# A hybrid attention block on one core: another order ahead of the first projection and around the first up unit, forget rows by one DMA, biases behind the first attention

## The chip, the cores and the metric

The kernel runs on one core of one Trainium2 chip. The metric is the device time of one execution in microseconds (us); lower is better. Every time below is of one launch with all inputs in DRAM.

## The reference

One layer over 256 tokens of width 1024, batch 1, all in float32. What is computed:

```python
h = rmsnorm(x, norm_mix)
proj = einsum('bsd,de->bse', h, w_in)          # q, k, v of three branches, 8 forget logits, 3 gates
o_a = stick_breaking_attention(q_a, k_a, v_a)  # 8 heads of 64
o_b = forgetting_attention(q_b, k_b, v_b, f_b + b_forget)   # adds c[q] - c[k], c a running sum
o_c = moba_attention(q_c, k_c, v_c, slopes)    # one block of 256 keys here: causal with ALiBi
lifted = einsum('bsnw,nwd->bsnd', branches, w_branch)
mixed = sum(sigmoid(g) * lifted, axis=branches)
x = x + mixed @ w_out
h = rmsnorm(x, norm_mlp)
hid = square(relu(h @ w_up))                   # 4096 features
x = x + hid @ w_down
out = rmsnorm(x, norm_final)
```

## The kernel before, in words

**Products.** Each float32 operand is split into a high part (`hi`, the value copied to the matmul's reduced float type) and a low part (`lo`, the rest), and a product is the sum of hi*hi, hi*lo and lo*hi. A weight tile is made in three steps by `pump` (L104): a DMA on SyncE's queue brings 1 MB into `raw` (two buffers), ScalarE (ACT) copies each half to `whi` (L122), VectorE (DVE) subtracts for `wlo` (L125). There are seven buffers of each, so `pump` runs up to seven halves ahead of `used` (L132), which TensorE's stages call when a half is spent. The first two halves are made otherwise: GpSimd (POOL) makes `whi_qa` of both (L124), DVE the first `wlo_qa`, POOL the second (L125).

**Order.** Up to the end of `proj_first` the program runs in the order in which it is written (`manual_schedule`). Behind it a scheduler orders each engine by what is ready in its model and by the order of the code; `follow` (L137) adds an edge that only keeps two instructions of one engine in order.

**Ahead of the first projection (L190 to L300).** TensorE runs twelve matmuls on zeros (L196) while the inputs load. For each of the two token tiles t = 0, 1, ACT and DVE sum squares (L232, L233), POOL takes the root (L246), and then DVE scales half of the tile (L278) and ACT the other half (L279). TensorE transposes the gains (L283) and then the scaled tiles, two feature blocks at a time and both token tiles of a block in turn (L288 to L293), and ACT and DVE write `hT` from the transposed blocks: hi by `gain_hi` (L256), lo by `gain_lo` (L260), eight of each. `proj_first` (L337) then runs 48 matmuls of 256 columns; the next stage is the `k` projection, `pqk<-hT,whi_ka`.

**Attention.** The steps of the three branches are interleaved by a table of events (L578 to L585) with the projections. `forget_terms` (L473) makes the running sums c, sends them to DRAM (`c_rows`, L498), and `forget_bias` (L508) brings two heads' rows back to all partitions by two DMAs of 128 KB (L513) and makes the biases of these two heads: ACT adds the row term (L519, four instructions), POOL masks (L521, four instructions). Four pairs of heads, so eight DMAs and sixteen ACT instructions. The biases are read by `softmax_pair` of branch b.

**Output projection and first up unit.** `token_major("o", ...)` (L640, called at L695) runs `part` for units u: the first four for all four output tiles, the last four (`tail`) tile by tile, so that (t, e) = (0,0), (1,0), (0,1), (1,1) come out one after another, twelve matmuls of 512 columns each. Behind each, `mixed_in` (L677) adds the residual on DVE (L681, two instructions), and `transpose_in` (L686) of the tile before runs on TensorE; with t = 1 comes `split_gain`, four `gain_hi` on ACT and four `gain_lo` on DVE into `h2`. The transposes of (1,1) stand inside the first of sixteen up units (L715), between its first sixteen matmuls (features 0 to 511) and the rest. The other up units run without a break; `token_major("d", ...)` follows, and the last norm.

The program's names: `ptr` is a transposed tile in PSUM, `pu` an up unit's sum, `ptok` a tile of a token-major projection, `x` in that stage the residual, `h` the normed activations `h2`.

Of the kernel before, what the change touches and what calls it, by code (L numbers as in the profile page):

```python
# [14 lines left out]
P = 128  # L15
S = 256
# [9 lines left out]
WARM = 12  # L26
# [11 lines left out]
def hybrid_attention_block(ctx, tc, x, norm_mix, w_in, b_forget, w_branch, w_out,  # L38
# [65 lines left out]
    def pump(up_to=None):  # L104
        while state["next"] < min(2 * len(plan), state["used"] + HALVES, up_to or 2 * len(plan)):
# [26 lines left out]
    def used(n=1):  # L132

        state["used"] += n
        pump()

    def follow(later, earlier):  # L137

        tc.add_manual_dep(later.ins, earlier.ins.name, mybir.DependencyInfo(
            mybir.DependencyClass.NoSync, mybir.DependencyReason.DATA), reason="order on one engine")  # L140
# [30 lines left out]
    def joined(p, o):  # L171

        nc.scalar.activation(p, o[:, 1], AF.Copy)
        nc.vector.tensor_tensor(p, o[:, 0], p, op=ALU.add)
# [20 lines left out]
    for i in range(WARM):  # L195
        nc.tensor.matmul(pw, idle[:, 0:P], idle, start=True, stop=True)  # L196
# [32 lines left out]
    def square_sum(src, junk, ss):  # L229

        n = src.shape[-1] // 2
        nc.scalar.activation(junk[:, 0:n], src[:, 0:n], AF.Square, accum_out=ss[:, 0:1])  # L232
        nc.vector.tensor_tensor_reduce(junk[:, n:], src[:, n:], src[:, n:], 1.0, 0.0, ALU.mult, ALU.add, ss[:, 1:2])  # L233

    def total_square(src, junk, so_far=D * EPS):
# [3 lines left out]
        square_sum(src, junk, ss)  # L239
# [14 lines left out]
    def gain_hi(pt, k0, g, hi):  # L254
        for i, k in enumerate((k0, k0 + 1)):
            nc.scalar.activation(hi[:, k], pt[:, i].rearrange("p t q -> p (t q)"), AF.Copy, scale=g[:, k:k + 1])  # L256

    def gain_lo(pt, k0, g, hi, lo):
        for i, k in enumerate((k0, k0 + 1)):
            nc.vector.scalar_tensor_tensor(lo[:, k], pt[:, i].rearrange("p t q -> p (t q)"), g[:, k:k + 1],  # L260
                                           hi[:, k].bitcast(F32), op0=ALU.mult, op1=ALU.subtract)

    def split_gain(pt, k0, g, hi, lo):
        gain_hi(pt, k0, g, hi)
        gain_lo(pt, k0, g, hi, lo)
# [5 lines left out]
    h_hi, h_lo = hT[:, :, 0], hT[:, :, 1]  # L271
    hs = []
# [508 lines left out]
```

## Time and profile before

| what | value |
|---|---|
| median of 3 runs | 461.76 us (460.93 to 462.1) |
| the profiled execution's own time | 460.2 us |
| its span, first to last instruction | 458.5 us |
| TensorE matmul (PE) | 446.5 us busy, 97% |
| VectorE (DVE) | 326.0 us, 71% |
| ScalarE (ACT) | 273.6 us, 60% |
| GpSimd (POOL) | 38.5 us, 8% |
| DMA | 80.71 MB, mean 176 GB/s |

In the rows, PE is TensorE's matmul, PEld its weight load, and SPq the DMA queue of SyncE. Times are in us from the span's start. The span is 1.7 us shorter than the execution's own time. A busy PE may still wait inside a group of matmuls; gaps between groups are listed as idle time.

### The profile page before, as it was taken

What the parts mean: (1) busy time and instruction counts of PE and PEld (TensorE: products, weight loads), DVE (VectorE), ACT (ScalarE), POOL (GpSimd) and SP (SyncE); (2) the same over time, 40 slices, a digit from 0 to 9 for tenths busy, and PEclk for the clock granted to TensorE, in tenths of its full rate; (3) what the DMA queues carried; (4) which work ended last, traced back from release to release, by engine and by line L of the source; (5) the groups of instructions that cost most, each with busy time, mean ns of one, the idle gap of its engine ahead of it and who ended that gap; (6) DMA issues with size and microseconds to landing.
All of it is one profiled execution on the core that took longest, in us unless ns stands there. A gap on an engine that the chain in (4) does not pass through costs nothing. (4 is left out here: it accounts for less than half of the span.)

```text
span 458.5 us, 6837 instructions
## 1 busy us (share of the span) xinstructions
PE 446.5 (97%) x2575; PEld 391.8 (85%) x2575; DVE 326.0 (71%) x543; ACT 273.6 (60%) x474; POOL 38.5 (8%) x75
## 2 busy tenths in 40 slices
PE   6999999999999999999999998999999999999993
PEld 3989998999899888888888887888888888888882
DVE  6878777888788878559759769877778864444425
ACT  5759997788567886556557446555556653334302
POOL 6503210213000000000000000000000000000012
PEclk9999999999999999999999999999999999999998
DMA  8768563445354448556556617766665576555202
GB/s 299 255 191 277 164 191 99 147 146 169 97 167 150 139 126 290 182 183 184 183 188 216 201 41 238 219 185 183 185 183 184 183 256 203 183 185 183 93 0 92
DMA packets 58002, 80.71 MB, mean 176 GB/s; under 512 B 2521, under 2 KB 45809, under 8 KB 57969
## 3 DMA queue, kind: packets, MB, share of 16 engines
q1 hardware_dynamic: 57632, 79.87, 54.1%
q8 instruction: 20, 0.33, 0.3%
q10 hardware_dynamic: 336, 0.40, 0.2%
q14 instruction: 14, 0.11, 0.1%
HBM read 79.21 MB, written 1.06 MB: 175 GB/s over the span
## 5 line engine op out<-in xcount | busy, mean ns | idle before, releaser
L125 DVE TENSOR_TENSOR wlo_d<-raw,whi_d 128x1024 fp32r<-128x1024 f32 x32 | 39.1, 1225 | 35.2 <-ACT whi_d L122 35.2
L151 PE MATMUL pu<-h,whi_u 128*128 128x512 f32 x256 | 61.4, 391 | 1.2 <-DVE h L260 1.2
L122 ACT ACTIVATE whi_d<-raw 128x1024 fp32r<-128x1024 f32 x32 | 33.8, 1059 | 42.3 <-PE ptok L151 34.2
L151 PEld LDWEIGHTS pu<-h,whi_u 128*128 128x128 f32 x256 | 46.9, 188 | 10.6 <-DVE h L260 1.5
L151 PE MATMUL ptok<-whi_d,u_lo 128*128 128x512 f32 x128 | 49.8, 389 | 0.0
L151 PE MATMUL ptok<-whi_d,u_hi 128*128 128x512 f32 x128 | 49.8, 389 | 0.0
L151 PE MATMUL pg<-hT,whi_g 128*128 128x512 f32 x192 | 46.7, 392 | 0.0
L122 ACT ACTIVATE whi_u<-raw 128x1024 fp32r<-128x1024 f32 x32 | 33.3, 1059 | 22.2 <-DMA raw<-in_w_up_dram 20.7
L125 DVE TENSOR_TENSOR wlo_u<-raw,whi_u 128x1024 fp32r<-128x1024 f32 x32 | 38.9, 1221 | 9.8 <-ACT whi_u L122 9.7
L151 PEld LDWEIGHTS pg<-hT,whi_g 128*128 128x128 f32 x192 | 35.1, 188 | 6.7
L125 DVE TENSOR_TENSOR wlo_g<-raw,whi_g 128x1024 fp32r<-128x1024 f32 x24 | 29.3, 1223 | 10.9 <-ACT whi_g L122 5.9
L151 PE MATMUL ptok<-wlo_d,u_hi 128*128 128x512 f32 x128 | 36.2, 389 | 0.0
L151 PEld LDWEIGHTS pu<-h,wlo_u 128*128 128x128 f32 x256 | 33.0, 191 | 1.3
L122 ACT ACTIVATE whi_g<-raw 128x1024 fp32r<-128x1024 f32 x24 | 25.4, 1058 | 14.3 <-PE pg L151 3.4
L151 PE MATMUL pu<-h,wlo_u 128*128 128x256 f32 x256 | 33.4, 283 | 0.0
L151 PEld LDWEIGHTS ptok<-whi_d,u_lo 128*128 128x128 f32 x128 | 24.0, 188 | 5.0
L151 PEld LDWEIGHTS ptok<-whi_d,u_hi 128*128 128x128 f32 x128 | 24.0, 188 | 5.0
L151 PEld LDWEIGHTS ptok<-wlo_d,u_hi 128*128 128x128 f32 x128 | 24.0, 188 | 5.0
L151 PEld LDWEIGHTS pg<-hT,wlo_g 128*128 128x128 f32 x192 | 25.1, 191 | 1.3
L151 PE MATMUL pg<-hT,wlo_g 128*128 128x256 f32 x192 | 25.5, 282 | 0.0
L739 POOL TENSOR_TENSOR xg<-x,g_fin 128x512 f32<-128x512 f32 x2 | 2.9, 1472 | 265.6 <-issue 264.2
L125 DVE TENSOR_TENSOR wlo_b<-raw,whi_b 128x1024 fp32r<-128x1024 f32 x12 | 14.7, 1223 | 10.5 <-PE pg L151 9.1
(498 smaller groups left out, 939.7 us busy)
## 6 DMA issues: line engine op xcount, KB each, us to landing
raw<-in_w_in_dram SPq DMA_DIRECT2D x29, 1024.0 KB, 5.0
raw<-in_w_up_dram SPq DMA_DIRECT2D x16, 1024.0 KB, 5.5
raw<-in_w_down_dram SPq DMA_DIRECT2D x16, 1024.0 KB, 4.8
raw<-in_w_branch_dram SPq DMA_DIRECT2D x6, 1024.0 KB, 5.0
raw<-in_w_out_dram SPq DMA_DIRECT2D x4, 1024.0 KB, 4.9
x_sb<-in_x_dram SPq DMA_DIRECT2D x2, 512.0 KB, 3.9
raw<-in_w_in_dram SPq DMA_DIRECT2D x2, 512.0 KB, 5.5
rows<-c_rows SPq DMA_DIRECT2D x8, 128.0 KB, 4.8
```

Source lines behind the costliest of these rows:

```text
L122: nc.scalar.activation(hi, raw, AF.Copy)
L125: (nc.gpsimd if n == 0 and i else nc.vector).tensor_tensor(lo, raw, hi.bitcast(F32), op=ALU.subtract)
L151: nc.tensor.matmul(o, l, r, start=first and i == 0, stop=last and i == len(pairs) - 1, **kw)
L739: nc.gpsimd.tensor_tensor(xg[:, d], x1[:, t, d], g_fin[:, d], op=ALU.mult)
```

## The change

1. **Ahead of the first projection.** Nine matmuls on zeros instead of twelve; the gains are transposed behind them, and six more matmuls on zeros stand behind that (`MORE`). The two DVE instructions that write `g_col` move ahead of the scaling of the tiles. The transposes run all of tile 0 first, then all of tile 1. POOL's `whi_qa` is made in halves of 512, and the first half gets a real wait for the last of DVE's scalings (`state["scaled"]`). The first `wlo_qa` on DVE is made in two halves as well. `proj_first` orders its 48 matmuls so that hi and lo weights alternate from the second feature block on.
2. **Forget rows.** One DMA of 1 MB brings the rows of all eight heads to all partitions, in `forget_terms`; `forget_bias` issues none. The ACT instructions of a bias follow `state["weighed"]`, the latest Exp of a stick-breaking pair at that point.
3. **Output projection.** `tail` is 3 instead of 4, and `used(tail)` behind the tail is gone; `used(3, ...)` stands in the first up unit behind `split_gain`, and `pump` takes two instructions (`behind`) that its first ACT and DVE instruction follow.
4. **First up unit.** The transposes of (1,1) move from behind sixteen matmuls to behind five.
5. **Up units.** `used` comes behind the reading of the sum, with the same `behind` edge; the sums of squares of the residual (L232, L233 at L726) follow the eighth unit.

```diff
-WARM = 12
+WARM = 9
+MORE = 6
...
-    def pump(up_to=None):
+    def pump(up_to=None, behind=()):
...
             if n:
-                nc.scalar.activation(hi, raw, AF.Copy)
+                made = nc.scalar.activation(hi, raw, AF.Copy)
+                rest = nc.vector.tensor_tensor(lo, raw, hi.bitcast(F32), op=ALU.subtract)
+                for later, earlier in zip((made, rest), behind):
+                    follow(later, earlier)
             else:
-                nc.gpsimd.tensor_scalar(hi, raw, 1.0, 0.0, op0=ALU.mult, op1=ALU.add)
-            (nc.gpsimd if n == 0 and i else nc.vector).tensor_tensor(lo, raw, hi.bitcast(F32), op=ALU.subtract)
+                halves = [slice(0, KD // 2), slice(KD // 2, KD)]
+                for ks in halves:
+                    made = nc.gpsimd.tensor_scalar(hi[:, ks], raw[:, ks], 1.0, 0.0, op0=ALU.mult, op1=ALU.add)
+                    if i == 0:
+                        follow(made, state["scaled"], mybir.DependencyClass.Sync)
+                for ks in halves if i == 0 else [slice(0, KD)]:
+                    (nc.gpsimd if i else nc.vector).tensor_tensor(lo[:, ks], raw[:, ks], hi[:, ks].bitcast(F32),
+                                                                  op=ALU.subtract)
...
+    warm(WARM)
...
+    pg = ps.tile([P, 2 * KD], F32, name="pg", tag="dense", bufs=3)
+    nc.tensor.transpose(pg, gains, ident[0:2 * KD, 0:2 * KD])
+    warm(MORE)
...
+        if t == 1:
+            nc.vector.tensor_scalar(g_mix, pg[:, 0:KD], ROOT_D, None, op0=ALU.mult)
+            nc.vector.tensor_copy(g_mlp, pg[:, KD:])
     for h, x_, rstd in zip(hs, x_sb, rstds):
-        nc.vector.tensor_scalar(h[:, 0:512], x_[:, 0:512], rstd, None, op0=ALU.mult)
+        state["scaled"] = nc.vector.tensor_scalar(h[:, 0:512], x_[:, 0:512], rstd, None, op0=ALU.mult)
...
-    for k0 in range(0, KD, 2):
-        pt = ptr("po" if k0 == 2 else "dense")
-        for t in range(NT):
-            transposes(hs[t], t, k0, pt)
-        pts.append(pt)
+    pts = [ptr("po" if k0 == 2 else "dense") for k0 in range(0, KD, 2)]
+    for t in range(NT):
+        for k0 in range(0, KD, 2):
+            transposes(hs[t], t, k0, pts[k0 // 2])
...
-        order = [(0, 0, 0, k) for k in range(4)] + [(0, 1, 0, k) for k in range(4)] + [(1, 0, 0, k) for k in range(4)]
-        order += [(j, a, 0, k) for k in range(4, KD) for j, a in ((0, 0), (0, 1), (1, 0))]
+        order = []
+        for k0, n in ((0, 2), (2, 2), (4, 1), (5, 1), (6, 1), (7, 1)):
+            order += [(0, a, 0, k) for a in range(2) for k in range(k0, k0 + n)]
+            if k0 == 2:
+                order += [(1, 0, 0, k) for k in range(4)]
+        order += [(1, 0, 0, k) for k in range(4, KD)]
...
-        rows = dram.tile([H, S], F32, name="c_rows")
-        nc.sync.dma_start(rows, minus_c)
+        c_rows = dram.tile([H, S], F32, name="c_rows")
+        nc.sync.dma_start(c_rows, minus_c)
+        rows = act.tile([P, H, S], F32, name="rows")
+        nc.sync.dma_start(rows.rearrange("p h q -> p (h q)"), c_rows.rearrange("h q -> (h q)").partition_broadcast(P))
...
-        pb = act.tile([P, 2, S], F32, name="rows", tag="rows", bufs=2)
-        for s in range(2):
-            nc.sync.dma_start(pb[:, s], rows[2 * pair + s].partition_broadcast(P))
...
-                nc.scalar.activation(b[:, t * P:t * P + n], pb[:, s, 0:n], AF.Identity, bias=cq[:, t, h:h + 1])
+                made = nc.scalar.activation(b[:, t * P:t * P + n], rows[:, h, 0:n], AF.Identity, bias=cq[:, t, h:h + 1])
+
+                follow(made, state["weighed"])
...
-        used(tail)
...
-    token_major("o", 8, m_hi, m_lo, 4, [(0, 0), (1, 0), (0, 1), (1, 1)], False, mixed_in)
+                state["split"] = split_gain(pts[i], 4 * e + 2 * i, g_mlp, h2[:, :, 0], h2[:, :, 1])
+
+    token_major("o", 8, m_hi, m_lo, 3, [(0, 0), (1, 0), (0, 1), (1, 1)], False, mixed_in)
...
-            used()
-            joined(r[:, i], pu[i])
+            state["read"] = joined(r[:, i], pu[i])
+            used(1, state["read"])
...
-            by_feature(pu, ws, h2, range(0, 4), last=False)
-            transpose_in(*waiting.pop(0))
+            for i in range(2):
+                for k in range(4):
+                    if (i, k) == (1, 1):
+                        transpose_in(*waiting.pop(0))
+                        used(3, state["split"])
+                    terms(pu[i].rearrange("p a q -> p (a q)"), [(ws[i][0][:, k], h2[:, k].rearrange("p a q -> p (a q)"))],
+                          k == 0, False)
+            for i in range(2):
+                terms(pu[i][:, 1], [(ws[i][1][:, k], h2[:, k, 0]) for k in range(4)], False, False)
             by_feature(pu, ws, h2, range(4, 8), first=False, done=done)
+        if u == 8:
+            middle = state["read"]
```

How the order moves, at three places. First DVE ahead of the first projection, from the root's input (`total`) to the lo parts of `hT`; `h` is the scaled token tile. Before:

```order
L241 SCALAR_TENSOR_TENSOR total<-ss 128x1
L278 TENSOR_SCALAR h<-x_sb,rstd 128x512 x2
L284 TENSOR_SCALAR g_col<-pg 128x8
L285 COPY g_col<-pg 128x8
L125 TENSOR_TENSOR wlo_qa_201<-raw_96,whi_qa_200 128x1024
L260 SCALAR_TENSOR_TENSOR hT<-ptr,g_col,hT 128x256 x8
```

And in the change:

```order
L259 SCALAR_TENSOR_TENSOR total<-ss 128x1
L302 TENSOR_SCALAR g_col<-pg 128x8
L303 COPY g_col<-pg 128x8
L305 TENSOR_SCALAR h<-x_sb,rstd 128x512 x2
L135 TENSOR_TENSOR wlo_qa_204<-raw_96,whi_qa_203 128x512 x2
L279 SCALAR_TENSOR_TENSOR hT<-ptr,g_col,hT 128x256 x8
```

The gains stand ahead of the scalings, and the lo part of the first weight tile is two instructions of half the size.

Second, DVE from the output projection into the first up unit. `x` is the residual sum of a `ptok` tile, `h` the lo part of `h2`, `wlo_u` the preparation of an up weight, ISA on `ys,ss` the sum of squares. Before:

```order
L125 TENSOR_TENSOR wlo_u_3043<-raw,whi_u_3042 128x1024
L681 TENSOR_TENSOR x_2970<-ptok,x_2970 128x256 x6
L260 SCALAR_TENSOR_TENSOR h_2975<-ptr,g_col,h_2975 128x256 x4
L125 TENSOR_TENSOR wlo_u_3127<-raw,whi_u_3126 128x1024
L681 TENSOR_TENSOR x_2970<-ptok,x_2970 128x256 x2
L125 TENSOR_TENSOR wlo_u_3133<-raw,whi_u_3132 128x1024
L125 TENSOR_TENSOR wlo_u_3137<-raw,whi_u_3136 128x1024
L233 ISA ys,ss<-x_2970 128x512
L233 ISA ss 128x1
L260 SCALAR_TENSOR_TENSOR h_2975<-ptr,g_col,h_2975 128x256 x4
```

And in the change:

```order
L124 TENSOR_TENSOR wlo_u_3055<-raw,whi_u_3054 128x1024
L703 TENSOR_TENSOR x_2966<-ptok,x_2966 128x256 x6
L279 SCALAR_TENSOR_TENSOR h_2971<-ptr,g_col,h_2971 128x256 x4
L703 TENSOR_TENSOR x_2966<-ptok,x_2966 128x256 x2
L279 SCALAR_TENSOR_TENSOR h_2971<-ptr,g_col,h_2971 128x256 x4
L124 TENSOR_TENSOR wlo_u_3154<-raw,whi_u_3153 128x1024
```

Between the last residual sums and the lo parts of `h2`, three weight preparations and a sum of squares have gone; the preparations stand behind.

Third, TensorE at the first up unit, from the transposes of (0,1) on. Before:

```order
L252 MATMUL ptr<-ident,x_2970 128x128 x4
L151 MATMUL pu<-h_2975,whi_u_3008 128x512 x4
L151 MATMUL pu<-h_2975,whi_u_3024 128x512 x4
L151 MATMUL pu<-h_2975,wlo_u_3009 128x256 x4
L151 MATMUL pu<-h_2975,wlo_u_3025 128x256 x4
L252 MATMUL ptr<-ident,x_2970 128x128 x4
L151 MATMUL pu<-h_2975,whi_u_3008 128x512
```

And in the change:

```order
L270 MATMUL ptr<-ident,x_2966 128x128 x4
L163 MATMUL pu<-h_2971,whi_u_3020 128x512
L163 MATMUL pu<-h_2971,whi_u_3004 128x512 x4
L270 MATMUL ptr<-ident,x_2966 128x128 x4
L163 MATMUL pu<-h_2971,whi_u_3020 128x512 x3
L163 MATMUL pu<-h_2971,wlo_u_3005 128x256 x4
L163 MATMUL pu<-h_2971,wlo_u_3021 128x256 x4
L163 MATMUL pu<-h_2971,whi_u_3004 128x512 x2
```

Eleven of the sixteen matmuls that stood ahead of the last transposes stand behind them.

## Rows read from the trace of the kernel before

**Rows 1.** The page: busy time, share of the span and instructions of each engine.
```profile
PE 446.5 (97%) x2575; PEld 391.8 (85%) x2575; DVE 326.0 (71%) x543; ACT 273.6 (60%) x474; POOL 38.5 (8%) x75
```

**Rows 2.** Waits of PE: who waited <- for whom, us in total, times, longest.
```profile
PE ptr L252 <- DVE h L278: 2.6, 2, 1.3
...
PE pu L151 <- DVE h L260: 1.2, 1, 1.2
```

**Rows 3.** Timeline, 0 to 24 us: start, us, engine, line, what, count [idle before].
```profile
3.78 0.15 PEld L196 LDWEIGHTS <-idle 128*128 128x128 bf16 x1 [0.28 <-issue]
4.21 0.78 PEld L196 LDWEIGHTS <-idle 128*128 128x128 bf16 x4 [0.28 <-issue]
...
6.44 0.48 DVE L278 TENSOR_SCALAR h<-x_sb,rstd 128x512 f32<-128x512 f32 x1
...
7.31 1.04 POOL L124 TENSOR_SCALAR whi_qa<-raw 128x1024 fp32r<-128x1024 f32 x1
...
7.36 1.27 DVE L278 TENSOR_SCALAR h<-x_sb,rstd 128x512 f32<-128x512 f32 x1 [0.45 <-POOL rstd L246]
8.55 0.15 DVE L284 TENSOR_SCALAR g_col<-pg 128x8 f32<-128x8 f32 x1
...
8.68 1.75 PE L252 MATMUL ptr<-ident,h 128*128 128x128 f32 x14 [1.27 <-DVE h L278]
8.69 1.21 DVE L125 TENSOR_TENSOR wlo_qa<-raw,whi_qa 128x1024 fp32r<-128x1024 f32 x1
8.82 1.99 POOL L124 TENSOR_SCALAR whi_qa<-raw 128x1024 fp32r<-128x1024 f32 x1 [0.47 <-DMA raw<-in_w_in_dram]
9.16 3.03 ACT L256 ACTIVATE hT<-ptr,g_col 128x256 fp32r<-128x256 f32 x8 [1.08 <-PE ptr L252]
10.04 3.23 DVE L260 SCALAR_TENSOR_TENSOR hT<-ptr,g_col,hT 128x256 fp32r<-128x256 f32 x8
...
10.90 2.41 POOL L125 TENSOR_TENSOR wlo_qa<-raw,whi_qa 128x1024 fp32r<-128x1024 f32 x1
...
16.28 2.08 PE L151 MATMUL pqk<-hT,whi_ka 128*128 128x256 f32 x16
...
18.20 1.12 PE L151 MATMUL pqk<-hT,wlo_ka 128*128 128x256 f32 x8
```

**Rows 4.** Timeline, 258 to 290 us, around the first up unit.
```profile
270.02 0.48 PE L151 MATMUL ptok<-whi_o,m_hi 128*128 128x512 f32 x1
...
270.96 1.66 DVE L260 SCALAR_TENSOR_TENSOR h<-ptr,g_col,h 128x256 fp32r<-128x256 f32 x4 [0.34 <-ACT h L256]
...
272.65 0.39 PE L151 MATMUL ptok<-wlo_o,m_hi 128*128 128x512 f32 x1
...
273.24 2.09 PE L151 MATMUL pu<-h,whi_u 128*128 128x512 f32 x8
273.78 0.75 DVE L681 TENSOR_TENSOR x<-ptok,x 128x256 f32<-128x256 f32 x2
...
276.12 0.60 PE L252 MATMUL ptr<-ident,x 128*128 128x128 f32 x4
276.54 1.57 ACT L256 ACTIVATE h<-ptr,g_col 128x256 fp32r<-128x256 f32 x4 [0.82 <-PE ptr L252]
...
277.41 1.66 DVE L260 SCALAR_TENSOR_TENSOR h<-ptr,g_col,h 128x256 fp32r<-128x256 f32 x4
...
277.95 2.32 PE L151 MATMUL pu<-h,whi_u 128*128 128x512 f32 x9 [1.23 <-DVE h L260]
```

**Rows 5.** Windows: us, busy of each engine (instructions), clock, DMA share, GB/s.
```profile
40.00:50.00 10.00, 10.00 (x81) 9.78 (x80) 8.71 (x12) 9.88 (x18) 3.56 (x7) 1.00 0.54 185
```

**Rows 6.** The tile `rows`: duration in ns, least, median, most, first and last start.
```profile
L519 ACT ACTIVATE bias<-rows,cq x16: 389/452/509, 41.2 to 98.3; 128x128 f32<-128x128 f32 x8, 128x256 f32<-128x256 f32 x8
```

**Rows 7.** Timeline, 24 to 62 us: a stick-breaking pair's lo part, and its reader.
```profile
49.60 0.96 DVE L382 TENSOR_TENSOR s_lo<-sp,s_hi 128x768 fp32r<-128x768 f32 x1
...
53.13 0.40 PE L424 MATMUL z<-s_hi,neg_tri 128*128 128x512 f32 x1
```

More of the change, by code (lines that the diff above doesn't have):

```diff
@@ L130, in weights, with used, follow @@
         return ready[which, br, j, i]
-    def used(n=1):
+    def used(n=1, behind=()):
         state["used"] += n
-        pump()
-    def follow(later, earlier):
+        pump(behind=behind)
+    def follow(later, earlier, kind=mybir.DependencyClass.NoSync):
         tc.add_manual_dep(later.ins, earlier.ins.name, mybir.DependencyInfo(
-            mybir.DependencyClass.NoSync, mybir.DependencyReason.DATA), reason="order on one engine")
+            kind, mybir.DependencyReason.DATA), reason="order")
     def mm3(o, lhs, rhs, first, last, **kw):
@@ L171, in joined @@
     def joined(p, o):
[L173 to L174 removed]
+        return nc.scalar.activation(p, o[:, 1], AF.Copy), nc.vector.tensor_tensor(p, o[:, 0], p, op=ALU.add)
     ramp = ExitStack()
@@ L194, in hybrid_attention_block, with warm @@
     pw = ps.tile([P, 512], F32, name="pw", tag="s2", bufs=2)
-    for i in range(WARM):
-        nc.tensor.matmul(pw, idle[:, 0:P], idle, start=True, stop=True)
+    def warm(n):
+        for i in range(n):
+            nc.tensor.matmul(pw, idle[:, 0:P], idle, start=True, stop=True)
+    warm(WARM)
     make_identity(nc, ident)
@@ L227, in hybrid_attention_block, with square_sum, total_square @@
                                 base=0, channel_multiplier=1)
-    def square_sum(src, junk, ss):
+    def square_sum(src, junk, ss, behind=()):
         n = src.shape[-1] // 2
-        nc.scalar.activation(junk[:, 0:n], src[:, 0:n], AF.Square, accum_out=ss[:, 0:1])
-        nc.vector.tensor_tensor_reduce(junk[:, n:], src[:, n:], src[:, n:], 1.0, 0.0, ALU.mult, ALU.add, ss[:, 1:2])
-    def total_square(src, junk, so_far=D * EPS):
+        a = nc.scalar.activation(junk[:, 0:n], src[:, 0:n], AF.Square, accum_out=ss[:, 0:1])
+        b = nc.vector.tensor_tensor_reduce(junk[:, n:], src[:, n:], src[:, n:], 1.0, 0.0, ALU.mult, ALU.add, ss[:, 1:2])
+        if behind:
+            follow(a, behind[0])
+            follow(b, behind[1])
+    def total_square(src, junk, so_far=D * EPS, behind=()):
         ss = small.tile([P, 2], F32, name="ss", tag="ss")
-        square_sum(src, junk, ss)
+        square_sum(src, junk, ss, behind)
         total = small.tile([P, 1], F32, name="total", tag="total")
@@ L428, in stick_pair @@
         w_ = act.tile([P, W768], F32, name="w_", tag="sp", bufs=2)
-        nc.scalar.activation(w_, zz, AF.Exp)
+        state["weighed"] = nc.scalar.activation(w_, zz, AF.Exp)
         parts = split768(w_, "w")
@@ L494, in forget_terms @@
         nc.vector.tensor_tensor_scan(c, ones_row, f, 0.0, ALU.mult, ALU.add)
-        minus_c = act.tile([H, S], F32, name="minus_c")
+        minus_c = act.tile([H, S], F32, name="minus_c", tag="bias", bufs=4)
         nc.vector.tensor_scalar(minus_c, c, -1.0, None, op0=ALU.mult)
-        rows = dram.tile([H, S], F32, name="c_rows")
-        nc.sync.dma_start(rows, minus_c)
+        c_rows = dram.tile([H, S], F32, name="c_rows")
+        nc.sync.dma_start(c_rows, minus_c)
+        rows = act.tile([P, H, S], F32, name="rows")
+        nc.sync.dma_start(rows.rearrange("p h q -> p (h q)"), c_rows.rearrange("h q -> (h q)").partition_broadcast(P))
         yield
@@ L725, in hybrid_attention_block @@
         v_ = small.tile([P, 1], F32, name="v_", tag="v_")
-        nc.vector.reciprocal(v_, total_square(x1[:, t], ys[:, t])[0])
+        nc.vector.reciprocal(v_, total_square(x1[:, t], ys[:, t], behind=middle)[0])
         nc.vector.tensor_scalar(v_, v_, float(D), None, op0=ALU.mult)
```

19 lines of the change are left out of this document (7 added, 12 removed).

## The prediction, made before the changed kernel was run

> **What bounds the kernel now.** I read the page first: TensorE is busy 446.5 of 458.5 us, the next engine (DVE) 326.0 [rows 1]. So the other engines matter only where TensorE waits for them. The list of TensorE's waits is short: 2.6 us in two waits of the transposes for the scaled tiles of DVE, and 1.2 us in the first up unit for the lo parts of `h2` [rows 2]. What is left idle is the first 1.2 us and the end behind the last matmul, and the change touches neither. A microsecond taken from one of these waits therefore comes off the end, unless TensorE catches up with another engine later.
>
> The timeline of the start shows why TensorE waits there. DVE scales half a tile in 0.48 us at 6.44, but the second tile's half takes 1.27 us from 7.36: POOL began its copy of `whi_qa` at 7.31 and held until 8.35, and DVE ended 0.28 us behind it [rows 3]. The transposes go on at 8.68. Then ACT writes eight hi parts of `hT` from 9.16 to 12.19 (9.16 + 3.03), DVE eight lo parts from 10.04 to 13.27, and the next stage begins at 16.28. A matmul of 256 columns costs 0.12 us there: sixteen lie between 16.28 and 18.20.
>
> The timeline of the up unit: the last residual sum starts at 273.78, although its `ptok` matmul began at 272.65; DVE was with a weight. The last transposes start at 276.12, ACT's hi parts at 276.54, DVE's lo parts at 277.41, and TensorE goes on at 277.95, after 1.23 us idle [rows 4].
>
> **The change, part by part.** *Head.* Six matmuls on zeros are added and three taken; they run in the gap before the transposes. Four take 0.78 us [rows 3], so six take 1.2 us and cost nothing as long as they end before the first scaled tile (6.92); if the gains came late, they would push the transposes by up to that 1.2. The two gain instructions go ahead of the scalings on DVE: 0.15 us together (they overlap; the second starts 0.07 after the first, and neither row is longer than 0.15), so the first tile is scaled at about 7.1. It does not delay the second tile, which waits for its root until 7.36. With POOL held back by the new wait, the second scaling takes 0.48 like the first: 7.36 to 7.84 instead of 8.63. The eight transposes of tile 0 run from about 7.1 at 0.11 us (1.75 / 14 is 0.125 with the last one's end in it), those of tile 1 from about 8.05. In the rows, ACT's first hi part starts 0.48 us behind the transposes that it waits for (8.68 to 9.16); now tile 1's first two are enough: 8.05 + 0.45 = 8.5, so 0.66 earlier. ACT's chain ends at 8.5 + 3.03 = 11.5.
>
> Behind the chain's end TensorE still has, in the new order, block 7 of the first half twice, four of the second half, sixteen with lo parts of `hT` and eight with `wlo` of the second half: 30 x 0.12 = 3.6, end 15.1. That is the best case, 1.15 us gained on 16.28. But the wait also moves POOL: its first half copy starts at 7.9 instead of 7.31, half a copy takes 0.52 (1.04 / 2), and half of `wlo_qa` on DVE 0.61 (1.21 / 2). The two compete: DVE's 1.21 from 8.69 ran at full speed and POOL's copy from 8.82 took 1.99 [rows 3]. If they take turns: POOL 7.9 to 8.95 for the first tile, DVE 9.0 to 9.6, POOL 9.6 to 10.15, DVE to 10.8, POOL to 11.3. DVE's eight lo parts then run from 10.8 to 14.0, TensorE uses each as it comes, and behind the last one it has two matmuls and the eight with `wlo`: 14.0 + 10 x 0.12 = 15.25. POOL's own `wlo` (2.41) is done at 13.7, in time. Gain 16.28 - 15.25 = 1.0. I take 1.0, with 1.15 as the upper bound; the lower one follows.
>
> The rows tell that whoever began first kept its speed. The Trainium skill says it as a rule: SBUF — State Buffer, section "Who interferes with whom", has GpSimd and a DVE instruction with two SBUF inputs share a port pair which the first to issue keeps for the whole instruction. The trace agrees in both directions. Between POOL's half copies lies no wait, though, and DVE must first be told that a half is there; so POOL could be first four times in a row: 7.9 + 4 x 0.52 = 10.0, DVE's halves to 11.2, lo parts to 14.45, end 15.65. That is a gain of 0.63, a rival below. With the late gains above, 1.0 less the part of 1.2 that is not hidden, I set the lower bound of the head at 0.3.
>
> *First up unit.* With three units in the tail a group is nine matmuls, not twelve; 270.02 to 272.65 is eleven steps of 0.24, so the last matmul of (1,1) would start 0.72 earlier against the group's start, at 271.9 on the old clock. DVE's lo parts for the first half end at 272.62 (270.96 + 1.66) and the residual sums follow at once to 273.4. TensorE, behind that matmul, has four transposes and five matmuls: 0.6 + 5 x 0.24 = 1.8 (in the rows the up unit starts 0.59 behind), so it reaches the last transposes at 273.7: no wait. ACT starts 0.42 behind them (276.12 to 276.54), at 274.15, and DVE 0.87 behind ACT (276.54 to 277.41), at 275.0; in the rows it is the same distance, though a sum of squares stood between, so I do not shorten it. The first lo part is done 0.5 later, at 275.5. TensorE has eleven matmuls as cover, 3 x 0.24 + 8 x 0.12 and the transposes' 0.5: 273.7 + 2.2 = 275.9. So the wait goes; what is late next has 0.4 to spare. The gain is the idle 1.23, and up to 0.25 more because restarting costs: 277.95 to 276.72 and the first matmul's longer step. I take 1.3, bounds 0.9 (0.4 of wait left) and 1.5.
>
> The three preparations that stood ahead of the split come behind it; they are of the third and fourth up unit and each costs ACT and DVE about 1.1 and 1.2 us. Done at about 280.5, they are needed after two units of some 5.3 us, from 273.24 on: not before 283. That is cover of 2.5 us. The sums of squares move to the ninth unit, where TensorE waits for nobody, and are needed at the end.
>
> *Rows and biases.* Bytes over the queue stay the same, but 1 MB comes at once near 34 us. Eight bias instructions of ACT, which all stood between 41 and 56 us, go behind the Exps of the third and fourth pair: 8 x 0.45 = 3.6 us less on ACT where it is busy 9.88 of 10 us [rows 5, 6]. TensorE does not wait there, so this gains nothing by itself. Its cover: a pair's lo part is ready at 50.56 (49.60 + 0.96) and read at 53.13, 2.6 us later [rows 7], and a TensorE that is 1.0 us earlier needs 1.0 of that. Biases of the first pair are read by DVE far later than they are now made, and I cost the move at nothing, between a gain of nothing and the rival's loss of the head.
>
> **The sum.** 1.0 + 1.3 = 2.3 off the profiled execution's 460.2 gives 457.9. The median shown, 461.76, is 1.56 above that execution, so I forecast 459.5 for the median. The unknowns span 0.3 + 0.9 = 1.2 to 1.15 + 1.5 = 2.65. A measurement of this kernel can tell about 0.3%, 1.4 us, from no change.
>
> **Rivals.** *POOL keeps the port:* worked out above, 0.63 + 1.3 = 1.9, 459.8. For it: no wait between POOL's halves. Against: DVE asks as soon as the first half is done, and got through at 8.69. Chance 0.10.
>
> *ACT becomes the bound and the head's gain is given back* in the first attention: TensorE, 1.0 us earlier, meets an ACT that was full there, or that waits at a `whi` copy whose `raw` the 1 MB delays. 1.3 is left, 460.5. For it 9.88 of 10 [rows 5]; against it the 3.6 us taken from ACT and the 2.6 us of slack [rows 6, 7]. Chance 0.14.
>
> *The up unit keeps its wait* (the change does not do what it says there): if DVE's lo parts come as late as now behind the transposes and the cover is 1 us short, say by late residual sums, some 0.4 is left of 1.3; with the head 1.4, 460.4. Chance 0.06.
>
> *Slower: the clock is low in the first projection.* The matmuls on zeros start at 0.43 us steps (3.78 to 4.21) and end at four in 0.78; 512 columns in 0.43 are 1.2 GHz, the lower of the two levels, and 0.2 is 2.4. In the rows the rise comes after eight of them, and it holds through idle times of 1.3 us. With nine and a gap for the gains it could fall again before the projection: then 48 matmuls of 256 columns take 0.21 instead of 0.12, 48 x 0.09 = 4.3 us more, which outweighs 2.3: 463.8. It decides if the clock is low at about 9 us and stays so for the 48. Against: six more matmuls stand in the very gap. Chance 0.04.
>
> **The numbers.** The forecast has 0.66, of which 0.05 for sums so near 1.2 that they count as no change. Faster: 0.61 + 0.10 = 0.71. Within 0.3%: 0.05 + 0.14 + 0.06 = 0.25. Slower: 0.04. The range goes down to 461.76 - 2.65, and 0.5 further because the three runs shown differ by 1.2: 458.6. Upward it takes in the two rivals at 460.4 and 460.5, with the same 0.5: 461.0. The clock rival is outside.
>
> **What would show it.** Right: the second scaling takes about 0.5 us, the `k` projection starts at about 15.3, no wait of TensorE for `h` in the first up unit, and none new between 40 and 60 us. The head is wrong if POOL's copies run through ahead of DVE's first `wlo_qa`, or the six matmuls push the transposes behind 7.1. The up unit is wrong if TensorE still idles behind its last transposes. The whole is wrong if both gains stand in the timeline and a new wait of TensorE behind 30 us takes them back.

## The result, and the profile after

The changed kernel takes 457.91 us, median of 6 runs (457.59 to 458.68); the kernel before, timed beside it, 461.24 us, median of 6 (459.76 to 462.1). The ratio is 0.9929, with a 95% interval of 0.9911 to 0.9947: faster by 3.3 us. The forecast was 459.5 with a range from 458.6 to 461.0; the result lies 0.7 us under the range. The two profiled executions lie only 2.39 us apart: 460.2 before, 457.81 after. The forecast difference for them was 2.3.

The page of the changed kernel, engines, beside [rows 1]:

```profile
PE 448.0 (98%) x2578; PEld 392.2 (86%) x2578; DVE 325.7 (71%) x544; ACT 273.3 (60%) x474; POOL 38.8 (9%) x77
```

TensorE's waits in the changed kernel, beside [rows 2]; this is the whole list:

```profile
PE pw L209 <- DVE idle L204: 1.2, 1, 1.2
```

Both waits of [rows 2] are gone; what is left is the start, which the change does not touch. The timeline of the head after, beside [rows 3]:

```profile
5.42 1.84 PE L209 MATMUL pw<-idle 128*128 128x512 bf16 x6
...
5.56 0.69 DVE L248 CUSTOM_DVE_ANT_0 h<-x_sb 128x512 f32<-128x512 f32 x1 [0.23 <-DMA x_sb<-in_x_dram]
...
6.59 1.09 DVE L305 TENSOR_SCALAR h<-x_sb,rstd 128x512 f32<-128x512 f32 x2
...
7.13 1.97 PE L270 MATMUL ptr<-ident,h 128*128 128x128 f32 x16
...
7.77 3.25 POOL L130 TENSOR_SCALAR whi_qa<-raw 128x512 fp32r<-128x512 f32 x4 [0.61 <-DVE h L305]
...
8.43 2.10 DVE L135 TENSOR_TENSOR wlo_qa<-raw,whi_qa 128x512 fp32r<-128x512 f32 x2 [0.75 <-POOL whi_qa L130]
8.48 3.04 ACT L274 ACTIVATE hT<-ptr,g_col 128x256 fp32r<-128x256 f32 x8 [0.56 <-PE ptr L270]
10.45 3.21 DVE L279 SCALAR_TENSOR_TENSOR hT<-ptr,g_col,hT 128x256 fp32r<-128x256 f32 x8
10.56 0.76 PE L368 MATMUL pqk<-hT,whi_qa 128*128 128x256 f32 x5
...
11.99 2.56 PE L368 MATMUL pqk<-hT,whi_qa 128*128 128x256 f32 x20
...
15.35 1.84 PE L163 MATMUL pqk<-hT,whi_ka 128*128 128x256 f32 x14
```

The `k` projection starts at 15.35 instead of 16.28: 0.93 gained. Matched one by one, TensorE's instructions stay 0.93 earlier up to the first up unit (272.30 beside 273.24), so nothing is given back in the attention. The up unit after, beside [rows 4]:

```profile
272.30 1.41 PE L163 MATMUL pu<-h,whi_u 128*128 128x512 f32 x5
273.55 0.60 PE L270 MATMUL ptr<-ident,x 128*128 128x128 f32 x4
...
275.63 2.09 PE L163 MATMUL pu<-h,whi_u 128*128 128x512 f32 x8
...
273.97 1.57 ACT L274 ACTIVATE h<-ptr,g_col 128x256 fp32r<-128x256 f32 x4 [2.55 <-PE ptr L270]
...
274.84 1.66 DVE L279 SCALAR_TENSOR_TENSOR h<-ptr,g_col,h 128x256 fp32r<-128x256 f32 x4 [1.81 <-ACT h L274]
276.52 3.50 DVE L124 TENSOR_TENSOR wlo_u<-raw,whi_u 128x1024 fp32r<-128x1024 f32 x3
```

No wait stands ahead of 275.63; 277.95 before less 0.93 is 277.02, so 1.4 more are gained here, and the total of 2.34 stays to the end.

So the profile pair is as forecast and the medians differ by 0.9 more. The six runs of the kernel before spread over 2.3 us, those of the change over 1.1. The experiments ask where those 0.9 us come from. **Theory A**: scatter, the pair is the whole effect. **Theory B**: the collision of POOL and DVE in the head costs more in other executions. **Theory C**: a wait in the attention that only some executions have. **Theory D**, formed when the first results came: the clock falls in the head in some executions.

### The profile page after: what moved, and what is told of

Read it like the earlier page. It is cut to its first block, busy times and chain, and to the rows that moved or that the text cites. A ratio compares the mean times of both kernels' runs of the same rounds, so it can differ in the third digit from the quotient of the medians.

```text
span 456.1 us, 6843 instructions
## 1 busy us (share of the span) xinstructions
PE 448.0 (98%) x2578; PEld 392.2 (86%) x2578; DVE 325.7 (71%) x544; ACT 273.3 (60%) x474; POOL 38.8 (9%) x77
## 5 line engine op out<-in xcount | busy, mean ns | idle before, releaser
L124 DVE TENSOR_TENSOR wlo_u<-raw,whi_u 128x1024 fp32r<-128x1024 f32 x32 | 38.8, 1222 | 11.5 <-ACT whi_u L123 11.1
```

The lines of the kernel that those rows point to most:

```text
L124: rest = nc.vector.tensor_tensor(lo, raw, hi.bitcast(F32), op=ALU.subtract)
```

## The experiments

**1. Each part alone.** First the kernel before again, unchanged.

> The kernel before, unchanged, to see how far its own executions lie apart. The two profiled executions differ by 2.39 us (460.2 to 457.81), the medians by 3.3 (461.24 to 457.91). Theory A (the profiles hold the whole effect; what is beyond it is scatter of the kernel before, whose six runs spread over 2.3 us): ratio 1.000, runs again between 459.7 and 462.1, with the lower end near 459.8. Theory B (a collision in the head ahead of the first projection costs the kernel before 1 to 2 us more in some executions than in the profiled one): the same ratio and spread, and the profile, if it is of a late execution, shows the k projection later than 16.28 us. Theory C (the waits that vary lie in the attention, by the forget rows): the same, with a late execution late behind 40 us only.

460.59 us median of 12 runs beside 461.59 of 35 of the same kernel, ratio 0.9986 (0.9972 to 0.9999): so a ratio this near 1 means nothing here, and two medians of one kernel can lie 1.0 us apart. Lowest runs 459.89 and 460.0. The run list gives what the medians hide: times come in groups, and each run's mean granted clock goes with them. Of the 35, those of 0.995 and more begin at 460.0, those of 0.992 lie mostly at 461.0 to 461.7, those of 0.989 to 0.990 at 462.7 to 463.4.

Then three kernels that undo all of the change but one part. The head alone (items 2 to 5 as before):

```diff
-        rows = act.tile([P, H, S], F32, name="rows")
-        nc.sync.dma_start(rows.rearrange("p h q -> p (h q)"), c_rows.rearrange("h q -> (h q)").partition_broadcast(P))
+            nc.sync.dma_start(pb[:, s], rows[2 * pair + s].partition_broadcast(P))
...
-    token_major("o", 8, m_hi, m_lo, 3, [(0, 0), (1, 0), (0, 1), (1, 1)], False, mixed_in)
+    token_major("o", 8, m_hi, m_lo, 4, [(0, 0), (1, 0), (0, 1), (1, 1)], False, mixed_in)
```

> The change ahead of the first projection alone; the forget rows, the output projection and the first up unit as before. All theories: k projection at 15.35 us instead of 16.28, so 0.93 less in the profile. Theory A: 0.93 less in the median too, ratio 0.998, and a spread of the runs of about 2 us, as before. Theory B: 1.5 to 2 us less in the median (ratio 0.996), and a spread of 1.1 us as in the changed kernel, since the collision is gone. Theory C: 0.93 less, spread of about 2 us.

461.88 us median of 12 (459.85 to 462.43), ratio 0.9994 (0.9977 to 1.0011): no gain at all. No clock under 0.994, but 7 of 12 runs stand at 461.8 to 462.4. The profiled execution is one of those. Its head keeps the length of the change (from the second square sum on `x_sb` at 6.35 to the `k` projection at 16.14 it is 9.79 us, as from 5.56 to 15.35), and then TensorE waits in the attention:

```profile
PE pw L209 <- DVE idle L204: 1.2, 1, 1.2
PE pu L163 <- DVE h L279: 1.2, 1, 1.2
PE po L156 <- DVE o__222 L422: 0.8, 1, 0.8
PE pqk L163 <- DVE pad_lo L338: 0.7, 1, 0.7
...
```

The timelines of the same execution show why: SyncE's queue, ScalarE and TensorE.

```profile
37.17 0.37 SPq L112 DMA_DIRECT2D raw<-in_w_in_dram  x1
37.59 3.72 SPq L535 DMA_DIRECT2D rows<-c_rows  x3
...
45.14 1.06 ACT L123 ACTIVATE whi_vb<-raw 128x1024 fp32r<-128x1024 f32 x1 [2.81 <-DMA raw<-in_w_in_dram]
...
48.06 2.14 PE L163 MATMUL pqk<-hT,whi_ka 128*128 128x256 f32 x16 [0.66 <-DVE pad_lo L338]
```

A weight load of 1 MB is issued at 37.17, three forget rows behind it on the same queue, and it lands when ScalarE goes on at 45.14: 8.0 us. In the profile of before it was issued at 36.66 and used at 42.62 without a wait:

```profile
36.66 0.37 SPq L111 DMA_DIRECT2D raw<-in_w_in_dram  x1
37.08 2.09 SPq L513 DMA_DIRECT2D rows<-c_rows  x3
...
42.62 1.05 ACT L122 ACTIVATE whi_vb<-raw 128x1024 fp32r<-128x1024 f32 x1
```

ScalarE, which is full there [rows 5], brings the delay to `pad_hi`, DVE's `pad_lo` and TensorE.

The output projection and up units alone (head and rows as before):

```diff
-WARM = 9
+WARM = 12
...
-    warm(MORE)
...
-        nc.sync.dma_start(rows.rearrange("p h q -> p (h q)"), c_rows.rearrange("h q -> (h q)").partition_broadcast(P))
+            nc.sync.dma_start(pb[:, s], rows[2 * pair + s].partition_broadcast(P))
```

> The change of the output projection and of the up units alone; the head and the forget rows as before. All theories: in the profile 1.41 us less at the first up unit and nothing ahead of it. Theories A, B and C: 1.4 less in the median, ratio 0.997. What tells them apart is the spread: about 2 us by B and C, since head and rows are as before; by A the same spread as in the other kernels, whatever it is.

459.17 us median of 12 (458.6 to 461.52), ratio 0.9959 (0.9943 to 0.9976). Six runs at 458.60 to 458.72, clock 0.996 to 0.998; five at 459.6 to 460.4, clock 0.994 or 0.995; one at 461.52, clock 0.987. 460.0, the lowest of the 35, less 458.6 is the 1.4 of the profile. Which loss the five show was not read from a trace.

The rows and biases alone:

```diff
-WARM = 9
+WARM = 12
...
-    warm(MORE)
...
-    token_major("o", 8, m_hi, m_lo, 3, [(0, 0), (1, 0), (0, 1), (1, 1)], False, mixed_in)
+    token_major("o", 8, m_hi, m_lo, 4, [(0, 0), (1, 0), (0, 1), (1, 1)], False, mixed_in)
```

> The forget rows by one DMA and the biases behind the first attention alone; head, output projection and up units as before. Theories A and B: no change, ratio 1.000, the starts of the matmuls as in the profile of the kernel before. Theory C: 0.9 to 1.0 us less in the median (ratio 0.998), with a spread of about 1 us.

460.46 us median of 12 (460.04 to 461.87), ratio 0.998 (0.9962 to 0.9997). Seven runs at 460.04 to 460.48, clock 0.995 or 0.996, and five at 460.96 to 461.87, all at 0.992. Not one run is late at a good clock. So the median fits theory C, though it is no further from 1 than that of the unchanged kernel allows, and the spread does not: the runs with a low clock are still there.

**2. The matmuls on zeros.** The change without the six:

```diff
-MORE = 6
+MORE = 0
```

> The changed kernel without the six matmuls on zeros behind the gains; all else as in the change. TensorE then has nothing to do from the gains (5.4 us) to the first transposes (7.1 us). Theory D (the kernel before lost time in some executions because the granted clock fell in this gap; the six matmuls prevent it): mean granted clocks of the runs again from 0.987 to 0.997 as in the kernel before and in the two kernels with its head, the runs under 0.994 some 0.8 to 3 us longer, median 458.7 to 459.5, spread 2 us or more. Theory A (the profiles hold the whole effect): the six matmuls cost and give nothing, median 457.9, spread 1.1 us, all clocks 0.996 to 0.997.

459.14 us median of 10 (458.0 to 460.24), ratio to before 0.995 (0.9933 to 0.9966): 1.2 above the change, spread 2.2. Theory A falls. The profiled execution (own time 460.14) shows the place; TensorE:

```profile
5.28 0.26 PE L293 MATMUL pg<-ident,gains 16*128 16x16 f32 x1
7.33 3.68 PE L270 MATMUL ptr<-ident,h 128*128 128x128 f32 x16 [1.80 <-DVE h L305]
...
11.66 0.63 PE L368 MATMUL pqk<-hT,whi_qa 128*128 128x256 f32 x2
12.09 0.63 PE L368 MATMUL pqk<-hT,wlo_qa 128*128 128x256 f32 x2
...
17.68 1.60 PE L163 MATMUL pqk<-hT,whi_ka 128*128 128x256 f32 x12
```

A window of the same execution (the clock is the third number from the end):

```profile
8.00:10.00 2.00, 2.00 (x12) 2.00 (x11) 1.37 (x2) 0.36 (x2) 1.85 (x3) 1.00 1.10 385
```

Behind 1.80 us of idleness the sixteen transposes take 3.68 instead of 1.97 us, and a matmul of 256 columns takes 0.21 us ((12.09 - 11.66) / 2), 1.2 GHz. The `k` projection starts 2.33 later than in the change (0.2 of it because the transposes start at 7.33 instead of 7.13), and nothing behind it differs. The granted clock, however, reads 1.00 in its windows from 0 to 20 us, and only one of the ten runs has a mean under 0.9935: the record misses this fall. The Trainium skill warns of it (TensorE: Matmul & The Clock Gate, the caveats behind "Seeing it yourself"): the recorded clock events have been seen to be unreliable. The trace agrees: 0.21 us a matmul beside a clock of 1.00.

The kernel before with only these matmuls as in the change:

```diff
-WARM = 12
+WARM = 9
+MORE = 6
...
+    warm(MORE)
```

> The kernel before with only the matmuls on zeros as in the change: nine, the gains, six more. Theory D: no run with a mean granted clock under 0.994; the many runs of the kernel before at 460.9 to 461.8 us with clock 0.992 and at 462.7 to 463.3 with 0.989 (20 of 35) vanish, the lowest runs stay at 460.0; median 460.0 to 460.5, but for late runs of another cause (7 of 35 in the kernel before). Theory A: runs, clocks and median as in the kernel before, 461.2 to 461.6.

460.38 us median of 12 (460.04 to 461.63) beside 461.19 of the kernel before (460.05 to 463.02, 21 runs), ratio 0.9989 (0.9976 to 1.0001). No clock under 0.995. The lowest runs do not move. By its interval the ratio alone does not decide; the clocks do. Over all runs, those with the six matmuls never show a mean clock under 0.9935 (0 of 71), those without in 54 of 118. A mean clock can miss a fall, as above, so the traces count too: in all nine profiles with the six matmuls the transposes run at the higher clock (sixteen in 1.91 to 1.97 us, or fourteen in 1.75).

**3. The two parts of the forget rows**, undone singly and together. Eight DMAs again, biases still held behind the first attention; then one DMA, biases free; then both undone:

```diff
-        nc.sync.dma_start(rows.rearrange("p h q -> p (h q)"), c_rows.rearrange("h q -> (h q)").partition_broadcast(P))
+            nc.sync.dma_start(pb[:, s], rows[2 * pair + s].partition_broadcast(P))
```

> The changed kernel with the forget rows by eight DMAs of 128 KB as before, the biases still behind the first attention. With the head alone, 7 of 12 runs were 2 us late at a good clock, and its profile shows a weight load of 1 MB, issued together with three row DMAs, that lands late, so that the weight copy of ScalarE waits 2.8 us for it. Theory E (the row DMAs beside the weight load on one queue make it land late): some of 12 runs, about half, 1.8 to 2.2 us above the others (459.8 to 460.3), at clocks of 0.994 or more; median between 457.9 and 460. Theory F (the biases on ScalarE are what is in the way): no such runs, median 457.9, spread 1.1 us.

458.28 us median of 6: four runs at 458.1 to 458.3, two at 459.30 and 459.36, at clocks of 0.995 and 0.997. That is not the half at 459.8 to 460.3 that theory E asked for, but it is not theory F's single group either: two runs are late by 1.1, and no trace shows by what. In the profiled execution, one of the four, TensorE does not wait.

```diff
-                follow(made, state["weighed"])
```

> The changed kernel without the edge that holds the biases behind the first attention; the rows still come by one DMA. Theory E: as the change, 457.9, spread 1.1 us. Theory F: late runs by 1 to 2 us, or a wait of TensorE between 40 and 70 us in the profile, median 458.5 to 460.

458.77 us median of 6 (458.63 to 459.3), and a small hole in TensorE's row where a pair's lo part is read, as theory F said: 52.90 to 53.29 is 0.39 for a matmul of 256 columns. Behind it TensorE is 0.37 later against the change than ahead of it.

```profile
52.90 0.28 PE L449 MATMUL z<-s_hi,neg_tri 128*128 128x256 f32 x1
53.29 0.50 PE L446 MATMUL z<-s_lo,neg_tri 128*128 128x512 f32 x1
```

> The changed kernel with the whole forget part as before: eight DMAs, and the biases not held behind the first attention. Undone singly, the DMA cost nothing that could be told (458.1 to 459.36) and the edge about 0.4 us (a wait of TensorE at 53 us). Theory G (either of the two is enough to keep the attention free; only both undone bring back the late weight load and the waits at 47 and 61 us that the head alone showed): runs in two groups, 457.6 to 458.7 and 460 or more, about half in the upper one, median 458.7 to 460.2. Theory A (rows and biases are worth nothing): 457.9, spread 1.1 us. The single edge's price alone: 458.3 to 458.8, no upper group.

459.67 us median of 9 (458.33 to 460.64), clocks 0.995 to 0.997. Three runs at 458.3 to 458.9, six at 459.5 to 460.6. The median and the spread are theory G's; its two groups are not so clear, for it wanted 460 or more in the upper one, and two runs reach that. So both undone together cost more than either, but that one alone is enough is not shown: with eight DMAs two of six runs were late. The profiled execution is one of the three, and TensorE does not wait in its attention; that the six are late as the head alone is late, above, is argued and not seen.

**4. POOL's wait** taken out of the change:

```diff
-                    if i == 0:
-                        follow(made, state["scaled"], mybir.DependencyClass.Sync)
```

> The changed kernel without POOL's wait for the last scaling; copies still in halves, gains first. By the prediction's reasoning (POOL's copy beside the second scaling makes it 1.27 instead of 0.48 us): in the profile the second scaling ends 0.3 to 0.8 us later where the raw tile lands before it starts, the k projection moves from 9.8 us behind the landing of the second token tile to 10.1 to 10.6 us behind it, median 458.3 to 458.7. Rival (with the gains moved ahead and the copy in halves the wait has nothing left to do, or the raw tile lands too late to collide, as at 7.5 us in the profile of the change): k projection 9.8 us or less behind that landing, median 457.6 to 457.9.

458.15 us median of 6 (458.01 to 458.43). DVE and POOL:

```profile
5.86 0.69 DVE L245 CUSTOM_DVE_ANT_0 h<-x_sb 128x512 f32<-128x512 f32 x1 [0.28 <-DMA x_sb<-in_x_dram]
...
6.89 1.45 DVE L302 TENSOR_SCALAR h<-x_sb,rstd 128x512 f32<-128x512 f32 x2
...
7.44 3.40 POOL L130 TENSOR_SCALAR whi_qa<-raw 128x512 fp32r<-128x512 f32 x4
```

And TensorE:

```profile
5.53 2.17 PE L206 MATMUL pw<-idle 128*128 128x512 bf16 x6
7.54 1.95 PE L267 MATMUL ptr<-ident,h 128*128 128x128 f32 x16
```

The collision is back: the two scalings take 1.45 together instead of 1.09. But the `k` projection starts at 15.74, 9.88 behind the square sum, against 9.79: 0.1 us, and the rival expected with this run is the nearer one. The collision costs next to nothing here. The second tile is scaled at 8.34 (6.89 + 1.45), and TensorE comes to it only behind the eight transposes of tile 0, at 8.4 (7.54 + 8 x 0.11). The 0.1 stands ahead of that: the six matmuls take 2.17 us here and 1.84 in the change, and the transposes start 1.68 behind the square sum instead of 1.57. From there to `k` it is 8.20 us here and 8.22 in the change.

**5. The two halves of the up unit's edit.** The place of the last transposes undone, then the order of the weight preparations:

```diff
-                    if (i, k) == (1, 1):
-                        transpose_in(*waiting.pop(0))
+            by_feature(pu, ws, h2, range(0, 4), last=False)
+            transpose_in(*waiting.pop(0))
```

> The changed kernel with the last transposes again behind sixteen matmuls of the first up unit; VectorE's and ScalarE's order (tail of 3, preparations behind the split) as in the change. By the rows of before, the lo part of the first block can end 1.2 to 1.3 us behind the start of the transposes when nothing stands before it, and the transposes take 0.6: TensorE waits 0.5 to 0.8 us. So 458.4 to 458.8 if both halves of this edit matter; 459.2 to 459.4 if the place does all of it; 457.9 if the order does.

459.51 us median of 8 (459.44 to 459.53). The wait of [rows 2] is back whole:

```profile
275.39 0.60 PE L270 MATMUL ptr<-ident,x 128*128 128x128 f32 x4
277.21 2.12 PE L163 MATMUL pu<-h,whi_u 128*128 128x512 f32 x8 [1.23 <-DVE h L279]
...
275.81 1.56 ACT L274 ACTIVATE h<-ptr,g_col 128x256 fp32r<-128x256 f32 x4 [4.20 <-PE ptr L270]
...
276.68 1.66 DVE L279 SCALAR_TENSOR_TENSOR h<-ptr,g_col,h 128x256 fp32r<-128x256 f32 x4 [3.44 <-ACT h L274]
```

DVE has been idle for 3.44 us and still starts 0.87 behind ScalarE, as in [rows 4]. So DVE's other work did not set the wait of before; the chain transposes, ScalarE, DVE did. The order alone is worth nothing.

```diff
-    token_major("o", 8, m_hi, m_lo, 3, [(0, 0), (1, 0), (0, 1), (1, 1)], False, mixed_in)
+    token_major("o", 8, m_hi, m_lo, 4, [(0, 0), (1, 0), (0, 1), (1, 1)], False, mixed_in)
...
+        used(tail)
-                        used(3, state["split"])
```

> The changed kernel with a tail of 4 and the weight preparations released behind the tail as before, the last transposes still behind five matmuls. If the order of VectorE's work matters beside the place, its preparations of 1.2 us each come ahead of the lo parts again and TensorE waits 0.3 to 1.4 us behind its first sixteen matmuls: 458.2 to 459.3. If the place does all of it: 457.9.

458.78 us median of 6 (458.78 to 458.88).

```profile
273.75 2.35 DVE L124 TENSOR_TENSOR wlo_u<-raw,whi_u 128x1024 fp32r<-128x1024 f32 x2
276.02 1.65 DVE L279 SCALAR_TENSOR_TENSOR h<-ptr,g_col,h 128x256 fp32r<-128x256 f32 x4
...
276.56 2.34 PE L163 MATMUL pu<-h,whi_u 128*128 128x512 f32 x9 [0.51 <-DVE h L279]
```

Now the preparations are in the way: TensorE's start goes from 275.63 to 276.56, of which 0.24 is the head of this execution (`k` at 15.59 instead of 15.35), so 0.7. The place alone gives 0.7 of the 1.4, the order the other 0.7, and only on top of the place.

**6. The kernel before, where it is late.** Two more profiles of it.

> The kernel before, unchanged, for a profile of an execution with a low mean granted clock (47 of its 84 runs so far lie under 0.9935; its two profiles at hand are of 0.996 and 0.998). Theory D: where the clock is 0.992, time 460.9 to 461.9, and the transposes and the first matmuls of the projection run at the lower level, as in the profile without the six matmuls (transposes 3.7 instead of 2.0 us), so that the k projection starts 1 to 2.5 us later than at 16.28; the rest of the program as in the first profile. Theory A: the loss is spread over the program and the head is as in the first profile.

> As the run beside it: a second chance for an execution of the kernel before with a low granted clock. Theory D: time and start of the k projection later by the same amount, 0.8 to 3 us. Where the clock is 0.995 or more: 460.0 to 460.5 and a head as in the first profile, or 461.8 and more with a late weight load at 42 to 45 us.

The second was a low one: own time 461.56, mean clock 0.992. Two windows of it, and TensorE:

```profile
8.00:10.00 2.00, 1.14 (x6) 1.14 (x7) 2.00 (x4) 0.67 (x3) 1.63 (x3) 0.62 1.10 384
10.00:12.00 2.00, 2.00 (x11) 2.00 (x11) 2.00 (x4) 1.97 (x6) 2.00 (x1) 0.53 1.07 400
```

```profile
7.15 0.44 PE L252 MATMUL ptr<-ident,h 128*128 128x128 f32 x2 [1.11 <-DVE h L278]
8.87 3.20 PE L252 MATMUL ptr<-ident,h 128*128 128x128 f32 x14 [1.27 <-DVE h L278]
```

The granted clock is 0.62 and 0.53 there, the fourteen transposes take 3.20 instead of 1.75 [rows 3], and the `k` projection starts at 17.66: 1.38 late. That difference stays to the end, 1.37. Of it 0.18 is the landing of the second token tile, whose square sum starts at 5.74 instead of 5.56; 1.2 is left for the clock.

```profile
5.74 0.69 DVE L233 CUSTOM_DVE_ANT_0 h<-x_sb 128x512 f32<-128x512 f32 x1 [0.31 <-DMA x_sb<-in_x_dram]
```

TensorE had been idle for 1.11 and 1.27 us just ahead.

The first had a good clock (0.997) and own time 461.02. Its `k` projection starts where the first profile's does (16.27), but ScalarE waits for the weight load that stands beside the row DMAs, and TensorE is later by 0.2 behind 50 us and by 0.86 behind 70:

```profile
44.57 1.06 ACT L122 ACTIVATE whi_vb<-raw 128x1024 fp32r<-128x1024 f32 x1 [1.34 <-DMA raw<-in_w_in_dram]
...
67.09 0.47 PE L144 MATMUL po<-s_hi,v_hi 128*128 128x512 f32 x1 [0.39 <-DVE o__216 L400]
```

From that weight copy on, ScalarE's instructions are 1.95 later than in the first profile, up to 69 us and beyond TensorE's wait at 67. So the kernel before loses time in two ways that its first profile did not show, and each has a row of its own.

## Why the prediction failed

**The step that failed** is the one from the profiled execution to the median: "The median shown, 461.76, is 1.56 above that execution, so I forecast 459.5 for the median." It took those 1.56 us as something that the changed kernel keeps. The changed kernel's median lies 0.10 above its profiled execution (457.91 and 457.81). The 1.56 were losses of the kernel before in other executions: 1.2 by the clock in one that was caught, 0.86 by the late weight load in another. In the change no run shows the low clock, and no run of the six is later than the lowest by more than 1.1. Lowest run to lowest run (459.76 to 457.59) it is 2.2, near the forecast 2.3; the medians add what the losses cost on the average. How much that is can't be told closely, since two medians of the kernel before lay 1.0 apart (experiment 1); the runs do not divide the 0.9 us between the two losses.

**The two terms that were set to nothing** hold it. *The six matmuls* were costed only as something that might be late; without them the change takes 459.14, 1.2 above 457.91 in the median and 0.4 in the lowest run (458.0 and 457.59). These two were not timed side by side; by the ratios to the kernel before (0.995 and 0.9929) it is 1.0. The rival on the clock had the right mechanism on the wrong kernel: it was the kernel before whose clock could fall in the gap. *Rows and biases* "at nothing": undone in the change they cost 1.8 us of the median (459.67), 1.4 by the ratios (0.9959 and 0.9929). The two prices are of undoing one thing in the changed kernel; they are not shares of the 0.9 us and do not add up to it. The rival in which the attention takes the head's gain back, chance 0.14, is what the head alone does in 7 of 12 runs, and the change with both its edits does not.

**The head**: 1.0 forecast, 0.93 found, `k` at about 15.3 forecast and 15.35 found; the two scalings take 1.09 together, the second 0.49 of it, as said. But the nearness is in part luck. The sum's last term lets DVE's lo parts set the end (14.0, then ten matmuls), and its best case the end of ACT's hi parts (11.5, then thirty). The rows show neither. TensorE runs its last 40 matmuls ahead of `k` without a gap from 10.56 (40 x 0.12 is 4.8), while ACT's hi parts end at 11.52 and DVE's lo parts at 13.66, each before TensorE comes to it. What TensorE still waits for lies ahead of 10.56: its first eight matmuls, from 9.10 on, take 0.5 us more than 8 x 0.12. POOL meets the scaling only where `raw` lands early; in the second profile of the kernel before POOL starts at 8.13, behind a scaling of 0.48 us, and `k` still starts at 16.30, 10.47 behind the square sum. The collision is worth 0.25 by that (10.72 - 10.47, 16.28 - 5.56 being 10.72), and 0.4 by the profiles with the same scalings and transposes at 10.32 (rows alone, and the six matmuls alone). The rest of the head, gains first, tile by tile, halves, the order of the 48 matmuls, gives 0.5 to 0.7 together. They were not separated. So theory B falls: the collision is the smaller part of the head, and once the rest is changed, POOL's wait adds nothing that the runs show (experiment 4). That the six matmuls "cost nothing" holds for the profiled execution, though they take 1.84 us there and not 1.2; in that of experiment 4 they hold the transposes up by 0.1. The prediction words the port rule for DVE instructions with two SBUF inputs; the scaling reads one tile, and that it is held up too stands on the rows alone (1.27 beside 0.48). POOL's copies and DVE's halves took turns, as the sum had it, not four copies first: that rival fell.

**The up unit**: 1.3 forecast, 1.4 found. The forecast times, transposes at 273.7 and lo parts at 275.0, look like the found ones, 273.55 and 274.84, but they are on the clock of the kernel before, where the found ones are 0.93 later: 274.48 and 275.77. The forecast took 0.72 off for the shorter tail. The tail takes nothing off: each group has three matmuls fewer and the stage ahead of the groups has them more, so the up unit starts where it did (272.30 and 0.93 is 273.23, before 273.24). The gain came out all the same, since transposes, lo parts and the eleven matmuls that cover them moved together. That the 0.87 from ScalarE to DVE could not be shortened was right (experiment 5), and so was naming the preparations as part of the price.

**What stays open**: why the weight load beside the row DMAs is in use within 6.0 us of its issue in one execution and lands after 7.0 in another (37.61 to 44.57, the late profile of the kernel before) and 8.0 in a third; the three row DMAs behind it take 2.09, 2.64 and 3.72 us to issue there, in the same order, which does not tell which is the cause. Why the head alone is late in 7 of 12 runs at a good clock, and the kernel before above 461.4 us in 9 of 30. And how often the late load, rather than an unrecorded fall of the clock, makes those nine (of the 72 taken beside the experiments 30 have a mean clock of 0.9935 or more).

## What to carry to other kernels

A profile is one execution: where a kernel's runs spread by more than a change is worth, ask what the late ones do before you add their distance to the forecast, because the change may remove it. List each run's time beside its mean clock; groups at other clocks, and late groups at a good clock, are two different losses. An edit that takes nothing off the profiled execution (filler matmuls in a gap, work moved off a full engine) can still be what lets another edit keep its gain: here the head alone gave a ratio of 0.9994.

## What the runs showed that I had not expected

TensorE's clock fell behind an idle time of 1.1 to 1.8 us, in some executions of the same kernel and not in others. The two idle times of up to 1.3 us in the first profile [rows 2] had passed without it, and so did 1.71 us ahead of the transposes where the up units alone were changed (fourteen of them in 1.75 us). So the length of the idle time does not tell by itself whether the clock falls. The Trainium skill tells of such a difference between runs at the first rise (TensorE: Matmul & The Clock Gate, Part 1: the number of matmuls at the low clock changes from run to run of one kernel); the traces agree, with twelve matmuls on zeros that take 4.63 us in one profile of the kernel before and 5.21 in another:

```profile
1.25 4.63 PE L196 MATMUL pw<-idle 128*128 128x512 bf16 x12 [1.25 <-DVE idle L193]
```

```profile
1.25 5.21 PE L196 MATMUL pw<-idle 128*128 128x512 bf16 x12 [1.25 <-DVE idle L193]
```

And the landing of the second token tile moves the whole program: 9.79 us lie between its square sum and the `k` projection in the change and in the head alone, but that sum starts at 5.56 in one and 6.35 in the other.
